# Low parts of output-product operands on POOL, and the scan's part added by accumulating transfers

## The chip, the cores and the metric

The kernel runs on one core of a Trainium2 chip. The metric is the device time of one execution in microseconds (us). The engines are TensorE (PE, with PEld for its weight loads), VectorE (DVE), ScalarE (ACT), GpSimd (POOL) and SyncE (SP). SP, ACT and POOL issue DMA transfers; each works through its own instructions in order, so an issue that waits holds up what stands behind it.

## The reference

One layer of a hybrid encoder for 512 tokens of width 2048, in float32: a bidirectional state-space scan and a multi-head latent attention run side by side from one input projection, and are merged:

```python
merged = jax.nn.sigmoid(g_ssm) * (y @ w_proj_ssm) + jax.nn.sigmoid(g_attn) * (o @ w_proj_attn)
return x + merged @ w_out
```

Here `y` is the scan's output and `o` that of attention, both 512x2048, and the two projections are 2048x2048. A final RMSNorm follows. The change concerns the two projections and the sum `merged`; everything ahead of them and behind them stays as it is.

## The kernel before, in words

**Precision.** Every float32 operand is held as two parts that TensorE multiplies at full rate: a high part (ACT's cast to the rounded type, L458) and a low part, the difference of the two (DVE's subtraction, L459). Where the negative is wanted (S2), L461 and L462 do the same with a scale of -1. One product of blocks is then three chains of matmuls: high by high (L604), high by the weights' low part (L605), low by high (L606). The function `split_into` makes both parts of 128x1024 elements. For weights the parts are called `wh` and `wl`, three buffers each; for operands they are kept whole (`S__13339` is S4 of the scan, `S__13418` is S3, `x__13505` is x22, `S__13044` S1 and `S__13049` S2; of attention's operands `x__13780` is x11, `x__13860` x12, `S__13948` S1, `S__14218` S4, `S__14317` S3 and `x__14398` x22).

**Strassen products.** Each projection is done by seven block products instead of eight, for each half of its columns. An operand is one of the blocks x11, x12, x22 or a sum S1 to S4 of blocks, which transfers have formed in DRAM before. A product runs over four chunks of weights: for each, the raw weights (or a column X or Y, or a sum of them) are split into `wh` and `wl`, and 12 matmuls follow, 48 in a product. The order in the scan's projection (`wps`) is P1 and P2 of both halves first, then, for each half, P5 (S1), P6 (S2), P3 (S4), P7 (S3), P4 (x22). Attention's projection (`wpa`) has P1, P5, P6, P2, P3, P7, P4 for each half. During P5, DVE also forms the column sums X+=Y (L721), and during P7 of the scan X is added up with raw weights loaded at that moment (L725, loads at L729).

**Operands while products run.** A table of hooks says after which product an operand is loaded (`L`, `LP`) and split (`C`, `CP`). The raw halves come through SP into a ring of three buffers, the same ring through which the raw weights come (`wraw`, with operands' halves named `xraw`). A buffer is free again when its low part has been made.

**What sets the order.** A scheduler orders the instructions of each engine by due times that the code sets by priorities; a step that is pinned (`keep_in_program_order`, in `CP` and `LP`) keeps its place in the order of the code among the other pinned ones. The splits of S4, S3 and x22 in the scan's projection, and of x22 in attention's, are not pinned before the change; the others in the table are.

**Gates and the merge.** When a block of the scan's projection is complete, DVE multiplies it by its gate (fetched by POOL a few products before) and POOL stores it to DRAM (`ms_d`). When a block of attention's is complete, DVE multiplies it by its gate (L1463), adds the scan's block (L1464), which POOL had fetched beside the gate into a buffer `ms` (L1456), and one product later TensorE transposes the result (`turn`, L1469) for the last projection.

Of the kernel before, what the change touches and what calls it, by code (L numbers as in the profile page):

```python
# [11 lines left out]
F32 = mybir.dt.float32  # L12
# [3 lines left out]
ALU = mybir.AluOpType  # L16
# [56 lines left out]
def build(tc, a):  # L73
    nc = tc.nc
    act, dve, pool, pe = nc.scalar, nc.vector, nc.gpsimd, nc.tensor
# [34 lines left out]
    def scratch(name, n=SEQ):  # L110
        return dr.tile([P, n], F32, name=name)
# [6 lines left out]
    zs_d, gs_d, ga_d, ms_d = ([[scratch(f"{n}{t}_{b}") for b in range(4)] for t in range(TT)]  # L118
                              for n in ("zs_d", "gs_d", "ga_d", "ms_d"))
# [167 lines left out]
    def put(dst, t):  # L287
        act.dma_start(dst, t)
# [116 lines left out]
    def st(name):  # L405
        return gp.tile([P, SEQ], F32, tag="st", bufs=3, name=name)
# [46 lines left out]

    def split_into(hi_, lo_, raw, sign=1):
        if sign == 1:
            i = act.copy(hi_, raw)  # L458
            dve.tensor_sub(lo_, raw, hi_.bitcast(F32))  # L459
        else:  # L460
            i = act.activation(hi_, raw, AF.Copy, scale=-1.0)  # L461
            dve.scalar_tensor_tensor(lo_, raw, -1.0, hi_.bitcast(F32), ALU.mult, ALU.subtract)  # L462
        return i

    def view4(t):
        return t.rearrange("p (k t) -> p k t", k=4)
# [8 lines left out]
    class Ops:  # L475
# [5 lines left out]
        def load(self, which, in_order=False):  # L481
            self.raws[which] = [raw_load(self.src[which], q, in_order) for q in range(2)]

        def split(self, which, op, in_order=False):
            for q, t in enumerate(self.raws.pop(which)):
                ks = slice(4 * q, 4 * q + 4)
                i = split_into(op[:, 0, ks], op[:, 1, ks], view4(t), -1 if which == "S2" else 1)
                if in_order:
                    tc.keep_in_program_order(i)
            self.view[which] = lambda s, j, i: op[:, s, j, i * P:(i + 1) * P]  # L490
# [42 lines left out]
    def w_split(raw):  # L533
        with tc.high_priority(offset=AHEAD):
            h = wp.tile([P, 1024], F32R, tag="wh", bufs=3, name="wh")
            l = wp.tile([P, 1024], F32R, tag="wl", bufs=3, name="wl")
            split_into(h, l, raw)
        return h, l
# [17 lines left out]
    def sum_tile(tag):  # L556

        if tag == "kk" or tag == "u" and kk:
            return kk.tile([P, SEQ], F32, tag="kk", bufs=2, name=tag)
        return part_.tile([P, SEQ], F32, tag=tag, bufs=2, name=tag)  # L560
# [11 lines left out]
    def after(n, f):  # L572
        later.append([n, f])
# [10 lines left out]
    def turn_bank(i):  # L584

        return SETS[used[1]][i]("turn")
# [24 lines left out]
    def product_rows(name, op, chunk, keep, each, pre):  # L611

        used.append((used[-1] + 1) % 4)
        bs = [b(name) for b in SETS[used[-1]]]
        for m in range(4):
            with tc.high_priority(offset=AHEAD):
                split_into(keep[0][:, m], keep[1][:, m], chunk(m))
        pre()
        for i in range(2):
            for j in range(8):  # L620
                xh, xl = op(0, j, i), op(1, j, i)
                wh, wl = (t[:, j // 2, j % 2 * 512:(j % 2 + 1) * 512] for t in keep)
                pe.matmul(bs[i], xh, wh, start=(j == 0), stop=False)
                pe.matmul(bs[i], xh, wl, start=False, stop=False)
                pe.matmul(bs[i], xl, wh, start=False, stop=(j == 7))
                yield 3
            each(i, bs[i])
# [791 lines left out]
    def place(shape, name, dt=F32R):  # L1419

        n = n_places[0] % 5
        n_places[0] += 1
        return xb.tile(shape, dt, tag="opb" if n else "opc", bufs=4 if n else 1, name=name)

    def slot(which):
        if which in ("x11", "x12"):
            return xa.tile([P, 2, 8, 256], F32R, tag="opa", bufs=2, name=f"{which}_")
        return place([P, 2, 8, 256], f"{which}_")

    y_ops, o_ops = Ops(yn_d), Ops(o_d)  # L1430

    def L(ops, w):
        return lambda: ops.load(w)

    def LP(ops, w):

        return lambda: ops.load(w, True)

    def C(ops, w):
        return lambda: ops.split(w, slot(w))  # L1440

    def CP(ops, w):

        return lambda: ops.split(w, slot(w), True)

    fetched = {}

# [4 lines left out]
    def fetch_pa(t, b):  # L1452
        fetched[t, b] = st("gate")
        pool.dma_start(fetched[t, b], ga_d[t][b])
        fetched["m", t, b] = sum_tile("ms")
        pool.dma_start(fetched["m", t, b], ms_d[t][b])  # L1456

    def done_ps(t, b, o):
        dve.tensor_mul(o, o, fetched.pop((t, b)))
# [1 line left out]

    def done_pa(t, b, o):
        dve.tensor_mul(o, o, fetched.pop((t, b)))  # L1463
        dve.tensor_add(o, o, fetched.pop(("m", t, b)))  # L1464

        def turn():
            tp = turn_bank(t % 2)
            for i in range(4):
                pe.transpose(tp[:, i * P:(i + 1) * P], o[:, i * P:(i + 1) * P], ident)  # L1469
            if b < 2:  # L1470
                o_ = st("turned")
                act.copy(o_, tp)
                d = m_d[f"x{t // 2 + 1}1"].rearrange("p (k t) -> p k t", k=8)
                put(d[:, 4 * b:4 * b + 4, t % 2 * P:(t % 2 + 1) * P], view4(o_))
            else:
                h, l = (m_op[f"x{t // 2 + 1}2"][:, s_, 4 * b - 8:4 * b - 4, t % 2 * P:(t % 2 + 1) * P] for s_ in range(2))
                act.copy(h, view4(tp))
                dve.tensor_sub(l, view4(tp), h.bitcast(F32))

        after(1, turn)  # L1480
# [3 lines left out]
    def m_place(*which):  # L1484
        def f():
            for w in which:
                op = m_op[w] = slot(w)
                m_ops.view[w] = lambda s, j, i, op=op: op[:, s, j, i * P:(i + 1) * P]
        return f
# [6 lines left out]
    def o_sums(n, i=1):  # L1496
        return lambda: [tc.keep_in_program_order(f()) for f in o_late[i][n]]

    wps = Strassen("wps", y_ops, -1, done_ps, fetch_ps, {
        (0, "P5"): [C(y_ops, "S4"), L(y_ops, "S3")],  # L1500
        (0, "P6"): [C(y_ops, "S3"), L(y_ops, "x22")], (0, "P3"): [C(y_ops, "x22")],
        (0, "P7"): [o_sums(2)], (0, "P4"): [LP(o_ops, "x11"), o_sums(3)],
        (1, "P5"): [CP(o_ops, "x11"), LP(o_ops, "x12"), o_sums(4)],
        (1, "P6"): [CP(o_ops, "x12"), LP(o_ops, "S1"), o_sums(5)],
        (1, "P3"): [CP(o_ops, "S1")], (1, "P7"): [LP(o_ops, "S2")], (1, "P4"): [CP(o_ops, "S2"), LP(o_ops, "S4")]})
    wpa = Strassen("wpa", o_ops, -1, done_pa, fetch_pa, {
        (0, "P1"): [CP(o_ops, "S4"), LP(o_ops, "S3")], (0, "P5"): [CP(o_ops, "S3"), LP(o_ops, "x22")],
        (0, "P6"): [C(o_ops, "x22")],
        (1, "P1"): [m_place("x11")], (1, "P5"): [m_place("x21")], (1, "P6"): [m_place("S1")],
        (1, "P2"): [m_place("x12"), L(m_ops, "x11")], (1, "P3"): [m_split("x11"), L(m_ops, "x21"), m_place("S2")],  # L1510
        (1, "P7"): [m_split("x21"), m_place("x22")], (1, "P4"): [m_place("S3")]})
# [7 lines left out]
    for hd in range(AH):  # L1519
# [24 lines left out]
        if hd == 12:  # L1544
            for w, tag in (("x11", "v_h"), ("x12", "v_l")):
                t = at.tile([P, TT, SEQ], F32R, tag=tag, bufs=2, name="yraw").bitcast(F32).rearrange("p a t -> p (a t)")
# [114 lines left out]
    for cg in range(2):  # L1661
        accs = [pa("f"), pa("f"), pb("f"), pb("f")] if cg == 1 else [mm("f"), mm("f"), mm("f"), pc("f")]
        for t in range(TT):
            o = res[t, cg] = sum_tile((("p1", "p5"), ("ms", "kk"))[cg][t // 2])
# [181 lines left out]
```

## Time and profile before

| | us |
|---|---|
| runs shown: median (lowest to highest) | 1981.22 (1973.48 to 1982.4) |
| profiled execution: time | 1973.34 |
| its span in the profile | 1971.6 |
| PE busy, idle in all | 1927.1, 44.5 |
| DVE busy | 1465.7 |
| ACT busy | 1028.9 |
| POOL busy | 249.3 |
| granted clock of TensorE | 0.998 |

Times in the profile count from the start of the span. The scan's projection runs from about 1470 us to 1635 us, attention's from there to about 1800 us. A row of a group gives the line, engine, operation, what is written and read, the shape and the count, then the busy time and the mean length of one in ns, and behind the last bar the engine's idle time just ahead of these instructions and what ended it. A row of the timeline begins with start and length in us.

### The profile page before, as it was taken

Reading aid. Unit: us, or ns where it says so; the run is one execution under the profiler, and the core shown is the slowest. Engines: PE = TensorE matmul, PEld = TensorE weight load, DVE = VectorE, ACT = ScalarE, POOL = GpSimd, SP = SyncE. Lnnn points to the kernel's source line nnn. Section 1 sums busy time; section 2 is a strip of 40 time slices with the busy share of each in tenths; the row PEclk is TensorE's granted clock in tenths of the full one; section 3 lists DMA queues with packets and bytes.
Section 4 is the critical chain, followed back from the end, with each engine's and each line's share of the span. In section 5 each row is a group of like instructions: output and inputs, shape, how many; then the busy total and the mean of one; then the engine's idle time right before and its main releaser. Section 6 shows DMA issues by size and latency. Waiting matters only on the chain.

```text
span 1971.6 us, 24488 instructions
## 1 busy us (share of the span) xinstructions
PE 1927.1 (98%) x8834; PEld 1590.0 (81%) x8834; DVE 1465.7 (74%) x2064; ACT 1028.9 (52%) x1527; POOL 249.3 (13%) x317
## 2 busy tenths in 40 slices
PE   7999999999999999999999999999999999999997
PEld 5888888888878888877788888888877787888886
DVE  7886676676759869788785557676776898879367
ACT  6444445444464856757747444444455455444353
POOL 0011001001112030030210211111021110100011
PEclk9999999999999999999999999999999999999999
DMA  6469669669654645665554867887388787847446
GB/s 216 167 203 255 165 167 245 155 179 246 144 175 146 202 125 162 205 206 189 158 159 139 243 176 201 210 222 201 105 217 309 235 280 276 281 157 242 168 85 161
DMA packets 170233, 383.27 MB, mean 194 GB/s; under 512 B 16704, under 2 KB 66944, under 8 KB 169920
## 3 DMA queue, kind: packets, MB, share of 16 engines
q1 hardware_dynamic: 103680, 234.02, 35.6%
q0 software_dynamic: 30912, 103.82, 23.5%
q10 hardware_dynamic: 35520, 43.87, 6.2%
q8 instruction: 69, 1.13, 0.2%
q14 instruction: 52, 0.43, 0.1%
HBM read 329.55 MB, written 98.17 MB: 217 GB/s over the span
## 4 chain that ended last, share of the span: by engine, by line
PE 78%; DVE 10%; DMA 6%; issue 3%; ACT 2%; POOL 0%; SPq 0%; ACTq 0%; DVEq 0%; POOLq 0%
PE P L605 11%; PE P L606 11%; PE P L604 11%; PE xbc L168 4%; PE xbc L169 4%; PE xbc L170 4%; PE za L170 2%; PE za L168 2%; PE za L169 2%; DVE sum L1135 2%; DVE wl L459 2%; PE qkv L168 1%; PE qkv L170 1%; PE qkv L169 1%; PE f L1613 1%
## 5 line engine op out<-in xcount | busy, mean ns | idle before, releaser
L458 ACT CAST wh<-X 128x1024 fp32r<-128x1024 f32 x164 | 172.4, 1054 | 197.6 <-PE P L606 149.6
L459 DVE TENSOR_TENSOR wl<-X,wh 128x1024 fp32r<-128x1024 f32 x164 | 199.7, 1222 | 85.7 <-ACT wh L458 85.2
L164 DVE TENSOR_TENSOR wl<-wraw,wh 128x1024 fp32r<-128x1024 f32 (+2 forms) x150 | 174.5, 1164 | 90.7 <-ACT wh L163 84.9
L163 ACT CAST wh<-wraw 128x1024 fp32r<-128x1024 f32 (+2 forms) x150 | 144.9, 967 | 121.6 <-PE xbc L169 34.4
L459 DVE TENSOR_TENSOR wl<-Y,wh 128x1024 fp32r<-128x1024 f32 x88 | 107.5, 1222 | 66.5 <-ACT wh L458 66.3
L458 ACT CAST wh<-Y 128x1024 fp32r<-128x1024 f32 x88 | 92.6, 1054 | 115.9 <-PE P L606 106.5
L168 PE MATMUL xbc<-h_h,wh 128*128 128x512 f32 x384 | 152.8, 398 | 0.0
L170 PE MATMUL xbc<-h_h,wl 128*128 128x512 f32 x384 | 149.8, 390 | 0.0
L169 PE MATMUL xbc<-h_l,wh 128*128 128x512 f32 x384 | 149.6, 390 | 0.0
L604 PE MATMUL P<-wh,h_h 128*128 128x512 f32 x384 | 149.4, 389 | 0.0
L605 PE MATMUL P<-wl,h_h 128*128 128x512 f32 x384 | 149.4, 389 | 0.0
L606 PE MATMUL P<-wh,h_l 128*128 128x512 f32 x384 | 149.4, 389 | 0.0
L458 ACT CAST wh<-wraw 128x1024 fp32r<-128x1024 f32 x68 | 71.7, 1055 | 110.6 <-PE P L606 60.1
L459 DVE TENSOR_TENSOR wl<-wraw,wh 128x1024 fp32r<-128x1024 f32 x68 | 83.0, 1221 | 59.7 <-ACT wh L458 59.7
L605 PE MATMUL P<-wl,S 128*128 128x512 f32 x288 | 112.1, 389 | 1.1 <-DVE wl L459 1.1
L604 PE MATMUL P<-wh,S 128*128 128x512 f32 x288 | 112.0, 389 | 0.0
L606 PE MATMUL P<-wh,S 128*128 128x512 f32 x288 | 112.0, 389 | 0.0
L170 PE MATMUL za<-h_h,wl 128*128 128x512 f32 x256 | 100.2, 391 | 2.5 <-DVE wl L164 2.5
L168 PE MATMUL za<-h_h,wh 128*128 128x512 f32 x256 | 101.5, 397 | 0.0
L169 PE MATMUL za<-h_l,wh 128*128 128x512 f32 x256 | 99.7, 389 | 0.0
L170 PEld LDWEIGHTS xbc<-h_h,wl 128*128 128x128 f32 x384 | 72.1, 188 | 15.6
L606 PEld LDWEIGHTS P<-wh,h_l 128*128 128x128 f32 x384 | 72.1, 188 | 15.0
(745 smaller groups left out, 5050.9 us busy)
## 6 DMA issues: line engine op xcount, KB each, us to landing
wraw<-wi SPq DMA_DIRECT2D x102, 512.0 KB, 3.7
T_wps<-wps POOLq DMA_DIRECT2D x32, 512.0 KB, 11.1
da<-da_d SPq DMA_DIRECT2D x64, 256.0 KB, 4.0
T_wpa<-wpa POOLq DMA_DIRECT2D x32, 512.0 KB, 9.3
wraw<-wps SPq DMA_DIRECT2D x24, 512.0 KB, 6.2
wraw<-wo SPq DMA_DIRECT2D x20, 512.0 KB, 3.6
xbc_d<-xbc ACTq DMA_DIRECT2D x24, 256.0 KB, 2.8
wraw<-wun SPq DMA_DIRECT2D x16, 384.0 KB, 5.2
```

What stands on the lines that cost most here:

```text
L163: act.copy(h, raw)
L164: dve.tensor_sub(l, raw, h.bitcast(F32))
L168: pe.matmul(out, wh, xh, start=start, stop=False)
L169: pe.matmul(out, wh, xl, start=False, stop=False)
L170: pe.matmul(out, wl, xh, start=False, stop=stop)
L458: i = act.copy(hi_, raw)
L459: dve.tensor_sub(lo_, raw, hi_.bitcast(F32))
L604: pe.matmul(bs[i], xh, wh, start=(j == 0), stop=False)
L605: pe.matmul(bs[i], xh, wl, start=False, stop=False)
L606: pe.matmul(bs[i], xl, wh, start=False, stop=(j == 7))
L1135: dve.tensor_tensor_scan(sums[-1], flat(da), mask, 0.0, ALU.add, ALU.mult)
L1613: pe.matmul(acc, mh, wh, start=(start and k == 0), stop=False)
```

## The change

`split_into` and `split` get an argument for the engine of the subtraction. A new hook `CQ` splits with the low part on POOL and the cast pinned. It takes the place of `C` and `CP` for S4, S3 and x22 of both projections and for x11, x12 and S1 of attention: nine operands of two halves, 18 subtractions of 128x1024. The loads of S3 in the scan's projection become pinned. S2 (with the scale of -1) stays on DVE. The scan's block is no longer fetched and added by DVE; an accumulating POOL transfer adds it from DRAM onto the finished block, after the gate's multiplication and ahead of the turn.

```diff
-    def split_into(hi_, lo_, raw, sign=1):
+    def split_into(hi_, lo_, raw, sign=1, by=dve):
         if sign == 1:
             i = act.copy(hi_, raw)
-            dve.tensor_sub(lo_, raw, hi_.bitcast(F32))
+            by.tensor_sub(lo_, raw, hi_.bitcast(F32))
...
-    def CP(ops, w):
-
-        return lambda: ops.split(w, slot(w), True)
+    def CP(ops, w, by=dve):
+
+        return lambda: ops.split(w, slot(w), True, by)
+
+    def CQ(ops, w):
+        return CP(ops, w, pool)
...
-        fetched["m", t, b] = sum_tile("ms")
-        pool.dma_start(fetched["m", t, b], ms_d[t][b])
...
-        dve.tensor_add(o, o, fetched.pop(("m", t, b)))
+        pool.dma_start(o, ms_d[t][b], accum_op=ALU.add)
...
     wps = Strassen("wps", y_ops, -1, done_ps, fetch_ps, {
-        (0, "P5"): [C(y_ops, "S4"), L(y_ops, "S3")],
-        (0, "P6"): [C(y_ops, "S3"), L(y_ops, "x22")], (0, "P3"): [C(y_ops, "x22")],
+        (0, "P5"): [CQ(y_ops, "S4"), LP(y_ops, "S3")],
+        (0, "P6"): [CQ(y_ops, "S3"), LP(y_ops, "x22")], (0, "P3"): [CQ(y_ops, "x22")],
...
-        (1, "P5"): [CP(o_ops, "x11"), LP(o_ops, "x12"), o_sums(4)],
-        (1, "P6"): [CP(o_ops, "x12"), LP(o_ops, "S1"), o_sums(5)],
-        (1, "P3"): [CP(o_ops, "S1")], (1, "P7"): [LP(o_ops, "S2")], (1, "P4"): [CP(o_ops, "S2"), LP(o_ops, "S4")]})
+        (1, "P5"): [CQ(o_ops, "x11"), LP(o_ops, "x12"), o_sums(4)],
+        (1, "P6"): [CQ(o_ops, "x12"), LP(o_ops, "S1"), o_sums(5)],
+        (1, "P3"): [CQ(o_ops, "S1")], (1, "P7"): [LP(o_ops, "S2")], (1, "P4"): [CP(o_ops, "S2"), LP(o_ops, "S4")]})
     wpa = Strassen("wpa", o_ops, -1, done_pa, fetch_pa, {
-        (0, "P1"): [CP(o_ops, "S4"), LP(o_ops, "S3")], (0, "P5"): [CP(o_ops, "S3"), LP(o_ops, "x22")],
-        (0, "P6"): [C(o_ops, "x22")],
+        (0, "P1"): [CQ(o_ops, "S4"), LP(o_ops, "S3")], (0, "P5"): [CQ(o_ops, "S3"), LP(o_ops, "x22")],
+        (0, "P6"): [CQ(o_ops, "x22")],
```

Three places show how the order moves. On DVE at the start of P5 in the scan's first half, before:

```order
L462 SCALAR_TENSOR_TENSOR S__13049<-xraw,S__13049 128x1024
L459 TENSOR_TENSOR S__13339<-xraw,S__13339 128x1024
L462 SCALAR_TENSOR_TENSOR S__13049<-xraw,S__13049 128x1024
L459 TENSOR_TENSOR wl<-X,wh 128x1024
L459 TENSOR_TENSOR S__13339<-xraw,S__13339 128x1024
L721 TENSOR_TENSOR X<-X,Y 128x1024
L459 TENSOR_TENSOR wl<-X,wh 128x1024 x2
```

And now:

```order
L462 SCALAR_TENSOR_TENSOR S__13049<-xraw,S__13049 128x1024 x2
L459 TENSOR_TENSOR wl<-X,wh 128x1024
L721 TENSOR_TENSOR X<-X,Y 128x1024
L459 TENSOR_TENSOR wl<-X,wh 128x1024
L679 TENSOR_TENSOR p_13243<-kk,P2b 128x512
```

The two halves of S4 no longer stand among P5's first weights. On ACT, from S2's casts to those of x22, before:

```order
L461 ACTIVATE S__13049<-xraw 128x1024
L458 CAST S__13339<-xraw 128x1024
L461 ACTIVATE S__13049<-xraw 128x1024
L458 CAST wh<-X 128x1024
L458 CAST S__13339<-xraw 128x1024
L458 CAST wh<-X 128x1024
L458 CAST S__13418<-xraw 128x1024
L458 CAST wh<-X 128x1024 x2
L458 CAST S__13418<-xraw 128x1024
L458 CAST x__13505<-xraw 128x1024
```

And now, where L567 is the eviction of P5's result:

```order
L461 ACTIVATE S__13049<-xraw 128x1024 x2
L458 CAST wh<-X 128x1024 x6
L567 COPY p_13335<-P_13257 128x512
L567 COPY p_13337<-P_13258 128x512
L458 CAST wh<-X 128x1024
L458 CAST S__13339<-xraw 128x1024 x2
L458 CAST wh<-X 128x1024
L458 CAST S__13418<-xraw 128x1024
L458 CAST wh<-Y 128x1024
L458 CAST S__13418<-xraw 128x1024
L458 CAST wh<-Y 128x1024 x3
L458 CAST x__13505<-xraw 128x1024 x2
```

S4's casts now follow P5's eviction, and S3's and x22's stand between the Y columns, which are P3's weights. On POOL, among the transfers for the sums of attention's operands, the gates and the stores of finished blocks, before:

```order
L1406 DMA o_S_221<-o_x_220 128x512
L1450 DMA gate<-gs_d_1_154 128x512
L1460 DMA ms_d_1_178<-ms 128x512
L1450 DMA gate<-gs_d_1_158 128x512
L1460 DMA ms_d_1_182<-ms 128x512
```

And now:

```order
L1406 DMA o_S_221<-o_x_220 128x512
L1453 DMA gate<-gs_d_1_154 128x512
L459 TENSOR_TENSOR S__13339<-xraw,S__13339 128x1024 x2
L459 TENSOR_TENSOR S__13418<-xraw,S__13418 128x1024 x2
L459 TENSOR_TENSOR x__13505<-xraw,x__13505 128x1024 x2
L1461 DMA ms_d_1_178<-ms 128x512
L1453 DMA gate<-gs_d_1_158 128x512
```

Six subtractions stand in a row ahead of the next store and the next gate's fetch. Those of x11, x12 and S1 stand in the same way in the second half, and those of attention's S4, S3 and x22 in a row ahead of the first accumulating transfer.

More of the change, by code (lines that the diff above doesn't have):

```diff
@@ L482, in load, with split @@
             self.raws[which] = [raw_load(self.src[which], q, in_order) for q in range(2)]
-        def split(self, which, op, in_order=False):
+        def split(self, which, op, in_order=False, by=dve):
             for q, t in enumerate(self.raws.pop(which)):
                 ks = slice(4 * q, 4 * q + 4)
-                i = split_into(op[:, 0, ks], op[:, 1, ks], view4(t), -1 if which == "S2" else 1)
+                i = split_into(op[:, 0, ks], op[:, 1, ks], view4(t), -1 if which == "S2" else 1, by)
                 if in_order:
```

## The prediction

> **What bounds the kernel now.** I read the page's busy times first, then the busy time of each engine in the stretch between the starts of the products that the change touches, then what TensorE waited for there, then the single rows in which POOL and DVE meet.
>
> ```profile
> span 1971.6 us, 24488 instructions
> PE 1927.1 (98%) x8834; PEld 1590.0 (81%) x8834; DVE 1465.7 (74%) x2064; ACT 1028.9 (52%) x1527; POOL 249.3 (13%) x317
> ```
>
> PE is busy for 98% of the span, so little is left to win: 44.5 us of idle time in all. The next view cuts the scan's and attention's output products at their starts: the columns are from and to, length, then busy time and count of PE, PEld, DVE, ACT and POOL, then clock, DMA share and GB/s. The rows are P5, P6, P3 and P7 of the scan's first half; P6, P3 and P7 of its second half; and P5, P6 and P2 of attention's first half.
>
> ```profile
> core 0: us, PE busy (x) PEld busy (x) DVE busy (x) ACT busy (x) POOL busy (x), PEclk, DMA share, GB/s
> 1518.68:1531.79 13.11, 11.59 (x50) 9.04 (x49) 13.11 (x14) 8.81 (x9) 0.95 (x2) 1.00 0.48 168
> 1531.79:1543.14 11.35, 11.19 (x50) 8.93 (x48) 9.11 (x9) 4.23 (x5) 3.05 (x5) 1.00 0.84 199
> 1543.14:1555.86 12.72, 11.45 (x50) 8.93 (x48) 9.39 (x10) 6.00 (x6) 0.00 (x0) 1.00 0.49 142
> 1555.86:1567.78 11.92, 11.35 (x50) 8.85 (x48) 8.53 (x10) 4.21 (x4) 1.18 (x3) 1.00 0.93 347
> 1590.27:1601.14 10.87, 10.87 (x49) 9.01 (x48) 9.53 (x9) 8.39 (x9) 2.42 (x4) 1.00 0.82 229
> 1601.14:1612.03 10.89, 10.89 (x50) 9.01 (x49) 9.99 (x11) 6.01 (x6) 0.00 (x0) 1.00 0.94 298
> 1612.03:1623.35 11.32, 11.32 (x50) 8.86 (x48) 9.65 (x11) 4.21 (x4) 1.13 (x2) 1.00 0.94 327
> 1646.42:1657.31 10.89, 10.89 (x50) 9.01 (x49) 10.31 (x10) 7.25 (x9) 0.00 (x0) 1.00 0.56 211
> 1657.31:1668.23 10.92, 10.92 (x49) 8.82 (x48) 8.96 (x8) 7.45 (x8) 0.00 (x0) 1.00 0.41 128
> 1668.23:1680.50 12.27, 11.48 (x50) 9.07 (x50) 12.27 (x14) 5.27 (x5) 0.00 (x0) 1.00 0.74 236
> ```
>
> An undisturbed product takes 10.88 us (48 matmuls; 10.87 to 10.89 in three rows), so a chunk of 12 matmuls, which needs one new `wl`, lasts 2.72 us. Over 10.88 stand P5 by 2.2 us, P3 by 1.8, P7 by 1.0 and P2 by 1.4; the ten rows lose 7.5 us together. That is the ceiling of any gain here, 0.4% of the span. DVE is busy for all of P5 and P2 and for 8.5 to 10.3 us elsewhere.
>
> ```profile
> L605 PE MATMUL P<-wl,S__13044 128*128 128x512 f32 x32 | 12.7, 396 | 1.5 <-DVE wl L459 1.5
> L605 PE MATMUL P<-wl,S__13339 128*128 128x512 f32 x32 | 12.6, 393 | 0.9 <-DVE wl L459 0.9
> L605 PE MATMUL P<-wl,S__13418 128*128 128x512 f32 x32 | 12.9, 404 | 0.6 <-DVE wl L459 0.6
> L605 PE MATMUL P<-wl,x__13505 128*128 128x512 f32 x32 | 12.7, 396 | 0.9 <-DVE wl L459 0.9
> ```
>
> Whenever PE stops here, a `wl`, the low part of the weights made by DVE, is what ended the wait (S__13044 is S1 of P5). DVE's order is therefore what bounds the stretch, and the change works on the right engine.
>
> **What a POOL low part costs.** No 128x1024 subtraction on POOL is in the trace. The nearest rows, of a start, a length and an instruction, except the last, which is a group:
>
> ```profile
> 573.51 1.26 POOL L1023 TENSOR_TENSOR c_l<-CT,c_h 128x512 fp32r<-128x512 f32 x1 [36.44 <-DMA xs<-xbc_d]
> 689.26 1.81 POOL L1023 TENSOR_TENSOR c_l<-CT,c_h 128x512 fp32r<-128x512 f32 x1 [68.91 <-ACT c_h L1022]
> 733.80 2.98 POOL L1088 TENSOR_TENSOR yo<-yo,tmp 128x512 f32<-128x512 f32 x2 [5.02 <-DVE tmp L1087]
> 735.56 2.31 DVE L164 TENSOR_TENSOR wl<-wraw,wh 128x1024 fp32r<-128x1024 f32 x1
> 871.37 2.56 POOL L1088 TENSOR_TENSOR yo<-yo,tmp 128x512 f32<-128x512 f32 x2
> 872.72 2.30 DVE L164 TENSOR_TENSOR wl<-wraw,wh 128x1024 fp32r<-128x1024 f32 x1 [2.19 <-ACT wh L163]
> L1370 POOL TENSOR_TENSOR small<-sm__9863 x1: 189/189/189, 1178.2 to 1178.2; 128x1 f32<-128x1 f32 x1
> ```
>
> c_l is the same operation at half the width, 1.26 us in the one that took least. A one-column instruction takes 0.19, so a doubled width is 0.19 + 2 x (1.26 - 0.19) = 2.33 us, which I take. The lowest it could be is 1.26 (if width cost nothing), the highest twice the 1.81 of the other c_l quoted, 3.6 (it has a wait in it). [...]
>
> The same rows show the second cost. In the pair at 733.80 POOL ends at 736.78 and the DVE split ends at 737.87, 1.09 us later; in the pair at 871.37 POOL ends at 873.93 and the split at 875.02, again 1.09 later. A split takes about 1.1 to 1.22 us, so both splits did nothing until POOL had finished: DVE and POOL take turns for whole instructions. [...] Moving a split to POOL therefore doesn't take it off DVE's time. It replaces a turn of 1.22 by one of 2.33.
>
> **The change, part by part.** Eighteen low parts leave DVE (9 operands of two halves) and become POOL instructions. Their times now:
>
> ```profile
> L459 DVE TENSOR_TENSOR S__13339<-xraw,S__13339 x2: 1217/1222/1226, 1516.8 to 1520.2; 128x1024 fp32r<-128x1024 f32 x2
> L459 DVE TENSOR_TENSOR S__13418<-xraw,S__13418 x2: 1212/1215/1218, 1535.1 to 1537.4; 128x1024 fp32r<-128x1024 f32 x2
> L459 DVE TENSOR_TENSOR x__13505<-xraw,x__13505 x2: 1220/1223/1226, 1538.5 to 1545.4; 128x1024 fp32r<-128x1024 f32 x2
> L459 DVE TENSOR_TENSOR x__13780<-xraw,x__13780 x2: 1217/1218/1219, 1593.2 to 1594.3; 128x1024 fp32r<-128x1024 f32 x2
> L459 DVE TENSOR_TENSOR x__13860<-xraw,x__13860 x2: 1217/1222/1226, 1596.6 to 1599.5; 128x1024 fp32r<-128x1024 f32 x2
> L459 DVE TENSOR_TENSOR S__13948<-xraw,S__13948 x2: 1215/1216/1216, 1606.4 to 1607.6; 128x1024 fp32r<-128x1024 f32 x2
> L459 DVE TENSOR_TENSOR S__14218<-xraw,S__14218 x2: 1217/1219/1221, 1649.6 to 1653.6; 128x1024 fp32r<-128x1024 f32 x2
> L459 DVE TENSOR_TENSOR x__14398<-xraw,x__14398 x2: 1218/1222/1226, 1660.0 to 1666.0; 128x1024 fp32r<-128x1024 f32 x2
> ```
>
> *P5, gain.* S4's two halves (1516.8 and 1520.2) stand today ahead of P5's first `wl` and of its first column sum. Pinned later, they leave that place: two turns of 1.22 less in a row full of DVE work. PE waited 1.5 us there for `wl`; I take a gain of 1.7 (bounds 1.5 and 2.2).
>
> *P6 and P3 of the first half.* ACT's order puts the casts of S4 behind P5's evictions, so S4, S3 and x22 all fall in these two products, six POOL turns of 2.33 = 14.0 us. DVE is busy for 9.11 + 9.39 = 18.5 us there, of which four splits (S3, x22) leave, 4.9. The turns add up to 27.6 us, against 24.1 us that the two products take today: +3.5. That is a floor, since turns alternate: a `wl` that is wanted every 2.72 us stands behind a turn of 2.33, and with the split itself (1.1) that is 3.4. Four POOL turns (S3, x22) stand in P3 alone, and each makes its chunk late by up to 0.7; two such are counted, 1.5. Together +5.
>
> *P6 and P3 of the second half.* x11, x12 and S1 stand here already, so six splits (7.3 us) leave and 14.0 come: 9.53 + 9.99 - 7.3 + 14.0 = 26.2 against 21.8, +4.4; with the same 1.5 for order, +6.
>
> *P7 of both halves.* The raw halves of operands share a ring of three buffers with the raw weights that P7 adds into X (L725), and a buffer is now given back by POOL.
>
> ```profile
> 1552.81 6.42 DMA wraw<-wps
> 1559.25 1.22 DVE L725 TENSOR_TENSOR X<-X,wraw 128x1024 f32<-128x1024 f32 x1 [3.60 <-DMA wraw<-wps]
> ```
>
> The first of these loads is issued at 1552.81 and lands at 1559.2, and DVE waits 3.6 us for it, with P7's third `wl` queued behind it. x22's last half is done at 1546.6 today; by six turns in a row it is done near the end of P3, up to 10 us later, and the second and third weight loads with it. I take +3 per P7 (bounds 0, if the queue's own earlier loads still set the time, and 6.4, a whole load): +6.
>
> *Attention's P5, P6 and P2.* S4, S3 and x22: 10.31 + 8.96 - 7.3 + 14.0 = 26.0 against 21.8 for P5 and P6: +4.2, say +4; P2 itself is full of DVE work and neither gains nor loses by it.
>
> *Accumulating transfers.* Sixteen loads of `ms` and sixteen DVE additions go, and sixteen accumulating POOL transfers come.
>
> ```profile
> L1464 DVE TENSOR_TENSOR p<-p,ms 128x512 f32<-128x512 f32 x12 | 8.2, 684 | 0.0
> ms<-ms_d POOLq DMA_DIRECT2D x16, 256.0 KB, 5.4
> big<-x POOLq DMA_DIRECT2D x8, 256.0 KB, 5.9
> L1688 POOL DMA_DIRECT2D big<-x x8 | 7.0, 1170 | 34.1 <-DVE big L737 27.2 <-DVE big L656 5.5 <-DVE big L651 1.5
> ```
>
> The additions are 16 x 0.68 = 11 us of DVE, after 1668 and with nothing waiting for them (0.0 idle behind), so I count no gain; the bound is P2's 1.4. The nearest accumulating transfer (`big<-x`) lands 5.9 us after its issue, and its issue takes 1.17: 7.1 us from the gate multiplication to the data. The turn comes one product later, 10.88 us: covered by 3.8. Where the second of a pair waits for a DVE turn that cover shrinks, and if it were gone the transfer would cost up to 7 us. I take +1 for the last of them.
>
> *Sum:* -1.7 + 5 + 6 + 6 + 4 + 1 = +20.3 us. The profiled execution took 1973.34 us (1971.6 of span and 1.7 around it), so 1993.6; I say 1993. The three runs shown go from 1973.48 to 1982.4 with a median of 1981.22: the profiled one is at their fast end, and a median may stand up to 8 us above my frame.
>
> **The rivals.** *Hidden.* A chunk has 2.72 - 1.22 = 1.5 us of slack. If a POOL turn took less than that, each would fit between two `wl`. The row at 573.51 is 1.26, so this holds if width costs little; one column at 0.19 speaks against it. Then the gain of P5 and the 1 of the transfers are left, with perhaps half of one P7: 1972 to 1979. Chance 0.18.
>
> *No turns, a gain.* If the subtraction of POOL ran beside DVE's, 18 splits and 16 additions would leave DVE for nothing, 33 us, and PE would win what it loses to `wl`: at most 7.5, 1966. The two meetings quoted speak against it. Chance 0.08.
>
> *Later still.* If the accumulating transfers land after the turn is due, in POOL's queue behind subtractions or slower than `big<-x`, each of eight pairs costs 2 or 3 us more: 1993 + 20 = 2013. It decides from a landing time of 10.9 us. Only attention's first pairs stand near POOL work, which speaks against it. Chance 0.1.
>
> **How the numbers follow.** The forecast itself (turns are exclusive, sum +10 to +30) has 0.64. Its own range is 1983 to 2005. The range takes in the upper end of "hidden" and most of "later still": 1975 to 2011. What a measurement of this kernel can tell from no change is about 0.5%, 9.9 us. Slower by more: 0.64 + 0.1, less a small part of the forecast that falls short, 0.73. Within: 0.19. Faster: 0.08.
>
> **What would show it.** A POOL L459 row near 2.3 us alone and near 3.4 behind a DVE split; DVE splits of 2 to 3.5 us in 1531 to 1690; PE idle before L605 in P3 and P7 of several us, where it is 0.6 to 0.9 now; P5's 13.1 us near 11.3. Wrong would be: POOL rows under 1.5 us; DVE splits staying at 1.22 beside POOL; P3 under 13 us in both halves. For the transfers: a `p<-ms_d` issue landing within 7 us, and PE not waiting at the turn's transposes.

## The result, and the profile after

The changed kernel takes 2006.87 us in the median of its runs, the kernel before 1978.27 in as many. The ratio is 1.0146, with a 95% interval of 1.013 to 1.0163: it is slower by 28.9 us. One of its five runs took 3975.4 us, and one run of an experiment below 5036.37 us; executions as far off as these are left out of the ratios. The forecast was 1993 with a range of 1975 to 2011 and slower as the likeliest side. The time is in the range, but the loss is about 1.4 times the sum of 20.3 us, and it is made up otherwise.

First the same rows as before, of the changed kernel: the head of its page with the span and the busy time of each engine, and then its stretches between the starts of products, in the prediction's order (P5, P6, P3, P7; P6, P3, P7; P5, P6, P2).

```profile
span 2005.4 us, 24491 instructions
PE 1940.6 (97%) x8834; PEld 1599.7 (80%) x8834; DVE 1460.2 (73%) x2030; ACT 1029.0 (51%) x1527; POOL 308.9 (15%) x335
```

```profile
core 0: us, PE busy (x) PEld busy (x) DVE busy (x) ACT busy (x) POOL busy (x), PEclk, DMA share, GB/s
1520.06:1530.94 10.88, 10.88 (x49) 8.89 (x48) 10.85 (x13) 4.81 (x5) 1.14 (x3) 1.00 0.47 164
1530.94:1542.58 11.64, 11.19 (x49) 8.93 (x48) 7.92 (x5) 6.38 (x8) 9.63 (x7) 1.00 0.65 135
1542.58:1559.16 16.58, 13.15 (x49) 9.90 (x48) 14.10 (x10) 7.98 (x8) 11.83 (x4) 0.90 0.62 190
1559.16:1570.04 10.88, 10.88 (x49) 9.01 (x48) 8.86 (x10) 4.22 (x4) 1.54 (x3) 1.00 1.00 379
1592.20:1603.20 11.00, 11.00 (x50) 8.93 (x48) 7.21 (x6) 8.38 (x9) 9.56 (x6) 1.00 0.57 151
1603.20:1620.20 17.00, 13.70 (x49) 10.52 (x48) 14.36 (x9) 6.21 (x6) 11.01 (x5) 0.82 0.75 234
1620.20:1631.54 11.34, 11.34 (x50) 9.31 (x48) 10.44 (x11) 3.90 (x4) 2.25 (x4) 0.96 0.99 368
1654.76:1667.13 12.37, 11.18 (x49) 8.94 (x48) 11.58 (x7) 7.07 (x8) 5.83 (x2) 1.00 0.56 207
1667.13:1680.11 12.98, 11.04 (x49) 8.82 (x47) 4.97 (x4) 7.43 (x8) 10.22 (x4) 1.00 0.32 103
1680.11:1694.95 14.84, 12.79 (x48) 10.24 (x49) 14.28 (x15) 5.26 (x5) 0.28 (x1) 0.89 0.66 208
```

Against the rows of before, P5 is 2.2 us shorter (10.88 instead of 13.11: it loses nothing any more) and P7 of the first half 1.0 shorter. P3 is 3.9 us longer in the first half (16.58 instead of 12.72) and 6.1 in the second (17.00 instead of 10.89). Attention's P5, P6 and P2 are 1.5, 2.1 and 2.6 longer. The 2.1 of P6 are in the main one stop at its very end, from 1678.17 to 1680.11, in which PE already waits for the first `wh` of P2. Note the clock: in P3 of the second half PE is busy for 13.70 us with work that takes 10.88 elsewhere, and the granted clock is 0.82. Of the 6.1 us lost there, 3.3 are idle and 2.8 are slow matmuls. The same slow stretch reaches into the P7 behind it (0.96).

How the turns of POOL and DVE look in P3 of the first half, in the changed kernel's timeline (start, length, instruction; first POOL, then DVE):

```profile
1535.81 5.83 POOL L459 TENSOR_TENSOR S__13339<-xraw,S__13339 128x1024 fp32r<-128x1024 f32 x2 [2.01 <-ACT S__13339 L458]
1541.61 6.72 POOL L459 TENSOR_TENSOR S__13418<-xraw,S__13418 128x1024 fp32r<-128x1024 f32 x2
1548.30 6.11 POOL L459 TENSOR_TENSOR x__13505<-xraw,x__13505 128x1024 fp32r<-128x1024 f32 x2
```

```profile
1546.00 1.27 DVE L737 TENSOR_TENSOR p<-p,P 128x512 f32<-128x512 f32 x2
1547.19 1.69 DVE L651 TENSOR_TENSOR p<-p,p 128x512 f32<-128x512 f32 x1
1548.81 3.37 DVE L459 TENSOR_TENSOR wl<-Y,wh 128x1024 fp32r<-128x1024 f32 x1
1552.11 2.85 DVE L651 TENSOR_TENSOR p<-p,p 128x512 f32<-128x512 f32 x1
```

POOL works without a gap from 1535.81 to 1554.41. A `wl` beside it takes 3.37 us instead of 1.22, and the small sum L651 takes 1.69 and 2.85 instead of 0.68. The two L737 ahead of them, which read one operand from PSUM (P), have POOL's subtraction of S3 beside them all the time and take 1.27 us together, no longer than without POOL (0.68 each in the mean before the change).

The two POOL low parts that DVE did not hold up are the last of attention's (x22, in a stretch in which DVE waited for a transfer). Their row among the changed kernel's POOL groups gives 2.37 us each, where the estimate was 2.33.

```profile
L459 POOL TENSOR_TENSOR x__14398<-xraw,x__14398 128x1024 fp32r<-128x1024 f32 x2 | 4.7, 2375 | 0.0
```

The other part of the loss is at the turns. Before the change PE never waited there; now it waits 12.9 us for the accumulating transfers, in four stops. These are the group rows of the kernel before and of the changed one, then the changed kernel's stretches of two of these turns (8 transposes) and of the products behind them:

```profile
L1469 PE MATMUL turn<-cst,p 128*128 128x128 f32 x48 | 6.2, 272 | 0.0
```

```profile
L1470 PE MATMUL turn<-cst,p 128*128 128x128 f32 x48 | 7.6, 290 | 12.9 <-DMA p<-ms_d 12.9
```

```profile
1705.83:1708.93 3.10, 1.01 (x9) 0.77 (x8) 2.46 (x3) 1.53 (x2) 0.00 (x0) 1.00 1.05 372
1708.93:1721.55 12.62, 12.62 (x51) 10.20 (x50) 5.27 (x7) 3.75 (x4) 2.91 (x4) 0.86 0.92 267
...
1733.34:1740.35 7.01, 1.36 (x9) 1.12 (x8) 3.00 (x5) 1.53 (x2) 1.73 (x3) 0.77 0.94 248
1740.35:1753.04 12.69, 12.69 (x50) 10.25 (x49) 5.58 (x6) 4.34 (x5) 1.44 (x2) 0.86 0.57 160
```

These two stops are paid twice: the product behind takes 12.6 to 12.7 us, all of it busy, at a granted clock of 0.86, where the same products take about 11.0 elsewhere. A third pair, from 1797.57, reads 4.20 and 12.59 us; behind the fourth stop, of 2.02 us, the product takes its usual 11.0. With three slow products, 12.9 + 3 x 1.6 = 17.7 us. The sum of what the rows lost in the products above is -2.2 + 0.3 + 3.9 - 1.0 + 0.1 + 6.1 + 1.5 + 2.1 + 2.6 = 13.4. Together that is 31, against 33.8 between the two profiled executions (2007.17 and 1973.34).

The four stops do not have one cause. Each ended when the second transfer of its pair landed. For that transfer, the table has the time from the end of the product that completed the block to the end of DVE's multiplication and to the issue on POOL, and then how long the landing took (us, from the changed kernel's timelines and its chain of waits):

| stop of PE, and its end | product's end | to multiplied | to issue | landing |
|---|---|---|---|---|
| 2.09, 1708.52 | 1694.95 | 4.4 | 4.7 | 8.8 |
| 5.65, 1739.59 | 1721.55 | 4.5 | 11.3 | 6.7 |
| 3.13, 1801.35 | 1786.58 | 3.3 | 4.5 | 10.3 |
| 2.02, 1816.98 | 1797.57 | 11.7 | 12.3 | 7.1 |

In the first and the third the landing is long. In the fourth the multiplication itself comes late. In the second, the longest, both are ordinary, but the issue stands 6.7 us behind the multiplication: on POOL a gate's fetch is ahead of it, and does not go before 1731.42.

```profile
1731.42 0.57 POOL L1457 DMA_DIRECT2D gate<-ga_d  x1 [7.14 <-issue]
1732.80 0.85 POOL L1465 DMA_DIRECT2D p<-ms_d  x1 [0.80 <-issue]
```

Gates and the turned blocks share one ring of three buffers in the program (`st`), and by the trace the store of a turned block landed at 1730.89, just before the fetch. Issued right behind its multiplication (1726.1), with the same 6.7 us, the transfer would by estimate have landed at 1732.8, ahead of the turn at 1733.34. No run takes this ring away, so this part is read from traces alone.

### The profile page after: what moved, and what is told of

It is laid out like the page before. It is cut to its first block, busy times and chain, and to the rows that moved or that the text cites. A ratio compares the mean times of both kernels' runs of the same rounds, so it can differ in the third digit from the quotient of the medians.

```text
span 2005.4 us, 24491 instructions
## 1 busy us (share of the span) xinstructions
PE 1940.6 (97%) x8834; PEld 1599.7 (80%) x8834; DVE 1460.2 (73%) x2030; ACT 1029.0 (51%) x1527; POOL 308.9 (15%) x335
## 4 chain that ended last, share of the span: by engine, by line
PE 78%; DVE 9%; DMA 5%; issue 5%; ACT 2%; POOL 1%; SPq 0%; ACTq 0%; POOLq 0%; DVEq 0%
PE P L605 10%; PE P L606 10%; PE P L604 10%; PE xbc L168 4%; PE xbc L169 3%; PE xbc L170 3%; PE za L170 2%; PE za L168 2%; PE za L169 2%; DMA p<-ms_d 2%; DVE sum L1135 2%; PE qkv L168 1%; PE qkv L170 1%; PE qkv L169 1%; PE f L1615 1%
## 5 line engine op out<-in xcount | busy, mean ns | idle before, releaser
L459 DVE TENSOR_TENSOR wl<-Y,wh 128x1024 fp32r<-128x1024 f32 x88 | 116.5, 1327 | 73.7 <-ACT wh L458 73.7
L605 PEld LDWEIGHTS P<-wl,h_h 128*128 128x128 f32 x384 | 72.1, 188 | 15.1
```

The costliest lines, as they stand in the source:

```text
L459: by.tensor_sub(lo_, raw, hi_.bitcast(F32))
```

## The experiments

Each ratio is against the kernel before, timed on the same chip, with its 95% interval; us are the ratio times 1975.5, about the median of the kernel before in these runs. The theory after the result had two independent parts, the turns of POOL on DVE's time and the landing of the accumulating transfers; the rivals were the sum on record, and the pinned order as the cause.

### The transfers alone

```diff
-        fetched["m", t, b] = sum_tile("ms")
-        pool.dma_start(fetched["m", t, b], ms_d[t][b])
...
-        dve.tensor_add(o, o, fetched.pop(("m", t, b)))
+        pool.dma_start(o, ms_d[t][b], accum_op=ALU.add)
```

> The kernel before, with the accumulating transfers alone: no load of ms, no DVE addition, sixteen accumulating POOL transfers; all low parts on DVE in the old order. Prediction's theory: +1 us, PE does not wait at the turn. Theory from the changed kernel's trace: PE waits at four or five of the eight turns for 2 to 6 us each and runs the next matmuls at half rate after each wait, together +12 to +18 us (ratio 1.006 to 1.009). Rival: the waits of the changed kernel came only because low parts on POOL made attention's first half late, then here +0 to +3 us.

Measured: ratio 1.0082 (1.0063 to 1.0101), +16 us. The transfers alone cost more than half of the whole loss, with no low part on POOL. PE waits 7.4 us at the turns by the row of its groups, and one product behind them again takes 12.6 us. These make 9.0 us in this one execution. It is 16.1 us longer than the profiled one of the kernel before, but 4.0 of these lie ahead of 1501 us, where nothing was changed.

```profile
L1467 PE MATMUL turn<-cst,p 128*128 128x128 f32 x48 | 7.3, 279 | 7.4 <-DMA p<-ms_d 7.4
```

The chain of waits of this run shows the worst place (start, length, what ran):

```profile
1769.96 0.61 DVE p L1461
1770.62 1.72 issue
1772.36 0.49 POOL p L1462
1772.91 0.41 POOL gate L1454
1773.45 10.29 DMA p<-ms_d
1783.79 0.72 PE turn L1467 x4
```

The product ended at 1768.95, so the turn was due at about 1779.9. The gate's multiplication comes 1 us after that end, the issue 3.4 to 4.5 us after it, and the landing takes 10.3 us.

### The low parts on POOL alone

The change with the two hunks above taken back.

> The change without the accumulating transfers: 18 low parts on POOL, the scan's part fetched and added by DVE as before. Prediction's theory: +19 us (ratio 1.0097), with 3 us each in P7 of both halves. Theory from the changed kernel's trace: +12 to +16 us, of which P3 of the two halves has 4 and 6 and attention's P5, P6 and P2 some 6, P5 of the scan gains 2, and P7 loses nothing. If the transfers were the whole cost: +0.

Measured: 1.0066 (1.0048 to 1.0084), +13 us, inside what the trace of the changed kernel gave and below the sum on record. P3 takes 16.20 and 17.13 us in this run, as in the changed kernel. With the run before it, 13 + 16 = 29 us, the whole loss: within the intervals, some 4 us for each, the two parts add up.

### The order without POOL

```diff
     def CQ(ops, w):
-        return CP(ops, w, pool)
+        return CP(ops, w, dve)
```

with DVE's additions put back.

> The same pinned order as the changed kernel, but every low part on DVE and the scan's part added by DVE. If POOL's turns are the cost of P3: -2 to +2 us, with P3 of both halves under 13 us. If the pinned order itself (S3 and x22 falling into P3) is the cost: +8 to +12 us, P3 near 16 us as in the changed kernel.

Measured: 0.9996 (0.9984 to 1.0009). The pinned order is not the cause. The rows of its stretches are P3 and P7 of the first half and P3 of the second:

```profile
1546.57:1557.61 11.04, 11.04 (x50) 8.93 (x48) 10.49 (x12) 7.41 (x8) 0.00 (x0) 1.00 0.72 223
1557.61:1572.23 14.62, 12.81 (x49) 10.07 (x48) 12.18 (x13) 4.20 (x4) 2.17 (x4) 0.88 0.88 315
1604.87:1615.75 10.88, 10.88 (x49) 9.01 (x48) 10.23 (x11) 6.02 (x6) 0.00 (x0) 1.00 0.90 303
```

P3 takes 11.04 and 10.88, as long as an undisturbed product. Most of what P5 and P3 of the first half gain, P7 gives back (14.62, before 11.92).

### Half as long turns

```diff
-            by.tensor_sub(lo_, raw, hi_.bitcast(F32))
+            if by is dve:
+                by.tensor_sub(lo_, raw, hi_.bitcast(F32))
+            else:
+                for k in range(2):
+                    by.tensor_sub(lo_[:, 2 * k:2 * k + 2], raw[:, 2 * k:2 * k + 2], hi_[:, 2 * k:2 * k + 2].bitcast(F32))
```

> As the kernel with low parts on POOL and DVE's additions, but each POOL low part is made by two instructions of half the width (about 1.2 to 1.3 us each instead of 2.35). If the length of one turn against a chunk's slack of 1.5 us is what makes weights late: most of the loss in P3 goes, +3 to +7 us over the kernel before instead of +12 to +16. If the summed time of the turns is what counts: no better than with whole instructions, +12 to +17.

Measured: 1.0056 (1.0039 to 1.0074), +11 us, not to be told from the +13 of whole instructions. In P3 of the first half the stop of 3.1 us is gone, two of 0.9 stand there instead, and P3 takes 13.37 us instead of 16.20. But P3 of the second half keeps a stop of 2.6 us (16.29), and while attention's P5 is 1.5 us shorter than with whole instructions, both P7 and attention's P6 and P2 are 0.4 to 1.0 longer. So shorter turns help in places but did not bring the total down to the +3 to +7 that the first of the two expectations gave. That the summed time of the turns is what counts would fit; why the time comes back elsewhere is not shown. In this run POOL's half instructions took 1.3 to 2.1 us in the mean of a group, where the shortest c_l of this width took 1.26 before; that they wait for DVE would fit (rows of its groups from 1500 to 1720):

```profile
L463 POOL TENSOR_TENSOR x__13509<-xraw,x__13509 128x512 fp32r<-128x512 f32 x4 | 8.4, 2139 | 0.0
L463 POOL TENSOR_TENSOR x__13868<-xraw,x__13868 128x512 fp32r<-128x512 f32 x4 | 5.0, 1300 | 0.0
```

### A transfer that nobody waits for

```diff
-        dve.tensor_mul(o, o, fetched.pop((t, b)))
-        pool.dma_start(o, ms_d[t][b], accum_op=ALU.add)
+        g = fetched.pop((t, b))
+        dve.tensor_mul(o, o, g)
+        pool.dma_start(g, ms_d[t][b], accum_op=ALU.add)
```

> As the kernel with accumulating transfers alone, but each transfer adds the scan's block onto the gate's buffer, which nobody reads any more, instead of onto the finished block; the scan's part is thereby left out of the sum. Same transfers, same DVE work, but the turn waits for the gate's multiplication only. If it is the wait for the landing that costs (and the slow matmuls behind each stop): the cost of 16 us goes, -2 to +3 us against the kernel before. If the transfers themselves disturb (POOL's queue, the gate buffers, DMA load): it stays at +10 to +16 us.

This kernel leaves the scan's part out of the sum. Measured: 1.0023 (1.0006 to 1.0039), +4.5 us instead of +16. The same transfers, issued at the same places, with the turn no longer waiting for them, as the group row of this run shows:

```profile
L1468 PE MATMUL turn<-cst,p 128*128 128x128 f32 x48 | 6.2, 272 | 0.0
```

So about 12 of the 16 us (16.2 - 4.5, each good to some 3.5) are the wait for the transfers and the slow matmuls behind it. The last 4.5 (1 to 8 by the interval) are above the expected -2 to +3 and stay unexplained. In the profiled execution 2.0 us stand in one product (12.98 from 1775.81, before 10.98): ACT waited 5.41 us there for a load (`xraw<-m_x`), and the next `wl` was late behind it. Whether the transfers held up this load is not shown.

### The three groups of low parts, one at a time

Each is the kernel before with one group by `CQ` and the other groups as they were.

The second group, x11, x12 and S1 of attention, was pinned already, so only the engine changes:

```diff
-        (1, "P5"): [CP(o_ops, "x11"), LP(o_ops, "x12"), o_sums(4)],
-        (1, "P6"): [CP(o_ops, "x12"), LP(o_ops, "S1"), o_sums(5)],
-        (1, "P3"): [CP(o_ops, "S1")], (1, "P7"): [LP(o_ops, "S2")], (1, "P4"): [CP(o_ops, "S2"), LP(o_ops, "S4")]})
+        (1, "P5"): [CQ(o_ops, "x11"), LP(o_ops, "x12"), o_sums(4)],
+        (1, "P6"): [CQ(o_ops, "x12"), LP(o_ops, "S1"), o_sums(5)],
+        (1, "P3"): [CQ(o_ops, "S1")], (1, "P7"): [LP(o_ops, "S2")], (1, "P4"): [CP(o_ops, "S2"), LP(o_ops, "S4")]})
```

> The kernel before with six low parts on POOL alone: x11, x12 and S1 of attention, which were pinned already and whose place in the order does not change. So only the engine differs. Theory of turns, by the trace of the changed kernel: P3 of the scan's second half loses 6 us, +5 to +8 us in all. By the sum on record, +6 in P6 and P3 and +3 in P7: +9. If the engine alone were harmless and the order were the cause: 0 to +2.

Measured: 1.0015 (1.0004 to 1.0027), +3 us: less than both theories gave. Its P3 and P7 in the second half:

```profile
1605.50:1622.00 16.50, 13.11 (x50) 10.00 (x49) 14.16 (x9) 6.40 (x7) 11.14 (x5) 0.90 0.76 232
1622.00:1632.88 10.88, 10.88 (x50) 9.01 (x48) 9.84 (x11) 4.22 (x4) 1.17 (x2) 1.00 0.98 374
```

P3 does lose 5.6 us, as in the changed kernel. Against that, what comes behind it is shorter: P7 takes 10.88 instead of 11.32, and P4 and attention's P1 and P2 gain 0.2 to 0.5 each, 1.5 in all. The 4 us that are left lie inside the interval (0.8 to 5.3). That a stop of PE gives the transfers in flight more time to land would explain the gain; no run shows it by itself.

The first group, S4, S3 and x22 of the scan:

> The kernel before with the first group of six low parts alone on POOL and pinned: S4, S3 and x22 of the scan. By the sum on record: -1.7 + 5 + 3 (P7) = +6.3 us. By the changed kernel's trace: P3 loses 4 us more than before, P5 gains 2, P7 gains up to 1: +1 to +3. If the three groups share the 13 us that all eighteen cost, with 3 for the second group: +4 to +5.

Measured: 1.0007 (0.9998 to 1.0016), +1.4 us, by the trace's estimate and not by the sum on record. In its trace P5 gains 1.4, P3 loses 3.9 and P7 gains 1.0.

The third group, S4, S3 and x22 of attention:

> The kernel before with the third group alone on POOL: S4, S3 and x22 of attention. By the sum on record: +4 us. By the changed kernel's trace, in which P5, P6 and P2 lose 1.5, 2.1 and 4.0 us against 0, 0 and 1.4 before: +6. If these waits came only because the groups ahead had made DVE late: +0 to +2.

Measured: 1.0039 (1.0025 to 1.0054), +7.7 us, the largest of the three; the groups ahead were not needed for it. The three groups give 1.4 + 3.0 + 7.7 = 12.1 us, the eighteen together 13. Why this one is worst is told by what SP's queue waited for in this run from 1640 to 1685 (in us, times, longest), and by DVE's timeline:

```profile
SPq L470 <- POOL S__14218 L459: 12.1, 2, 9.2
SPq L470 <- POOL S__14317 L459: 8.6, 1, 8.6
```

```profile
1650.27 3.31 DVE L721 TENSOR_TENSOR X<-X,Y 128x1024 f32<-128x1024 f32 x1
1653.51 3.40 DVE L459 TENSOR_TENSOR wl<-X,wh 128x1024 fp32r<-128x1024 f32 x1
...
1671.40 2.51 DVE L725 TENSOR_TENSOR X<-X,wraw 128x1024 f32<-128x1024 f32 x1 [5.47 <-DMA wraw<-wpa]
```

Two things happen. POOL's turns lengthen the column sum and a `wl` in P5 to 3.3 and 3.4 us. And SP waits 20.7 us with its next raw loads until POOL has given back a buffer of the ring; P2's first raw weights therefore land so late that DVE sits idle for 5.5 us. The trace tells them apart by place: P5 is 1.9 us longer than before, and PE stands still for 1.95 us at the end of P6, for P2's first `wh`, and for 2.02 in P2, for its `wl`. With the slow matmuls behind these stops (0.43 us each instead of 0.23, and a granted clock of 0.78 in P2), P6 and P2 are 5.5 us longer together. A larger ring, which would test this, was not tried.

### S4 alone, on either engine

```diff
-        (0, "P5"): [C(y_ops, "S4"), L(y_ops, "S3")],
+        (0, "P5"): [CQ(y_ops, "S4"), L(y_ops, "S3")],
```

> The kernel before with the two halves of the scan's S4 alone on POOL, pinned as in the change. P5 gains 2 us as in the changed kernel; P6, in which the two turns fall, has 9.1 us of DVE work in 11.35, less than S3's and x22's splits that stand there, so that two turns of 2.35 fill it: theory of turns -1 to +4 us. If turns on POOL cost nothing where only two fall into a product: -2.

Measured: 0.9999 (0.9986 to 1.0012). The same with `CP` in place of `CQ`, so on DVE:

> The kernel before with the scan's S4 pinned and split by DVE, nothing on POOL: the one part of the change that takes work out of P5's start. P5 gains 1.5 to 2 us. If that gain stays, -2 us; if P7 gives it back, as in the run with every pin and no POOL (P7 lost 3.75 us there, 1.0 before), -1 to +1.

Measured: 0.9993 (0.998 to 1.0006). Both do what the change wanted in P5 (PE's wait for `wl` in S1's products falls from 1.5 to 0.4 us with the pin), and neither moves the time beyond its interval. The gain is given back, but not in P7, as was expected (11.09 and 11.06 us, before 11.92): in both traces it is P4 of the first half that grows, from 11.61 to 16.39 and 14.03 us. The trace with POOL is that of the slowest of its twelve runs (1984.35, median 1976.5). Neither can be called faster than the kernel before; no version here beats it.

### The gate's multiplication first

```diff
-        dve.tensor_mul(o, o, fetched.pop((t, b)))
-        pool.dma_start(o, ms_d[t][b], accum_op=ALU.add)
+        with tc.high_priority(offset=AHEAD):
+            dve.tensor_mul(o, o, fetched.pop((t, b)))
+            pool.dma_start(o, ms_d[t][b], accum_op=ALU.add)
```

> As the kernel with accumulating transfers alone, but the gate's multiplication and the transfer are given the priority that weight splits have, so that DVE comes to them up to one or two instructions earlier. If the landing, 13 us and more after the product's end against 10.9, is late by the whole chain: the 16 us shrink by 1 to 4 us, and the turn still waits. If DVE's place for the multiplication is the whole cause: +3 us or less against the kernel before.

Measured: 1.0079 (1.0062 to 1.0096), +15.6 us: no change from +16. So a higher priority for the multiplication saves nothing. The test is a weak one: against the run with the transfers alone, the second multiplication of a pair comes 1 to 2 us earlier behind its product in five pairs and no earlier in the other three. The chain of this run's longest stop (3.31 us) has the wait of the gate's fetch for a buffer:

```profile
1696.32 5.53 DMA m_x<-turned
1702.42 0.09 POOL gate L1454
1702.97 6.88 DMA p<-ms_d
```

The multiplication was done at 1699.0, the transfer behind the gate's fetch was issued 4 us later, and it landed at 1709.86 for a turn that began at 1705.99.

## Why the prediction was right, and where its steps were wrong

**The direction and its reason.** The sum said slower, since a POOL low part is a turn of 2.33 us in place of one of 1.22. That held: 2.37 us where POOL was alone, 3.37 for a DVE split behind it, P3 of 16.6 and 17.0 us, and no loss in P3 when the same order runs without POOL. Not every DVE instruction beside POOL took longer: two L737, which have a PSUM operand, took 1.27 us together, as without POOL (0.68 each), and two L651 with both operands in SBUF took 1.69 and 2.85 instead of 0.68. In the prediction's reading of PE's waits, "whenever" was a little too much: 0.3 us ahead of the first half's P3 were ended by a `wh`.

**P5, -1.7.** Right: 13.11 to 10.88, -2.2.

**P6 and P3, +5 and +6.** About right as to place: +4.2 in the first half and +6.2 in the second, by the rows of the changed kernel. But a count of turns was only part of the reason: 3.4 and 3.3 us of the two P3 are idle time, and of what PE's work took beyond 10.88 (2.3 and 2.8 us) the larger part is due to the reduced clock behind the stop (0.90 and 0.82 over the two P3), which the prediction did not have.

**P7, +3 twice.** Wrong. The step failed where it made the second and third weight loads late "with" x22's last half: P7 lost nothing (10.88) or as much as before (11.34 against 11.32), because P3 itself had become longer and the loads landed within that time. In the first half DVE's wait for the first of them is 2.22 us instead of 3.60, and it lands 2.0 us after the start of P7 instead of 3.4. The ring of three buffers did cost time, in attention's P2, where the prediction counted nothing.

**Attention's P5, P6 and P2, +4.** Too small: 1.5, 2.1 and 2.6 in the changed kernel, 7.7 us for this group alone. The turns cost less than the +4 (P5's 1.5; P6's 2.1 are already the wait for P2's weights). The step "P2 itself neither gains nor loses" is the one that failed; its raw weights came late through the ring.

**Low parts in all.** The prediction's terms give -1.7 + 5 + 6 + 6 + 4 = 19.3; measured, 13.

**The accumulating transfers, +1.** The mis-sized term: 16 us. Its step of "7.1 us from the gate multiplication to the data", covered by 3.8, failed. (The 5.9 us in it run from the start of the issue, so that the 1.17 of the issue were counted twice; that error is on the safe side.) Four things were missing. First, the 10.88 us start at the product's end, not at the multiplication; in the changed kernel the pair's issues stand 3.4 and 4.7 us behind that end (1694.95), by its timeline of POOL:

```profile
1698.37 0.90 POOL L1465 DMA_DIRECT2D p<-ms_d  x1 [17.98 <-DVE p L1464]
1698.96 0.88 POOL L1457 DMA_DIRECT2D gate<-ga_d  x1
1699.69 1.05 POOL L1465 DMA_DIRECT2D p<-ms_d  x1
```

and the chain of waits has the landing of the second:

```profile
1699.69 8.79 DMA p<-ms_d
```

Second, this landing took 8.8 us where 5.9 was taken from `big<-x`, the median of eight landings from 4.3 to 8.2 us at another time of the kernel (the median of the new transfers onto `p` is 6.8). 4.7 + 8.8 = 13.5 us, against the 10.9 at which the turn is due. Third, POOL's order: a gate's fetch that waits for a buffer holds up the transfer behind it, as in the stop of 5.65 us. Fourth, behind three of the four stops the next matmuls were slow (a granted clock of 0.86 over the product). The rival "later still" had the mechanism (a landing past 10.9 us, through POOL's queue or a slower transfer), but got a chance of 0.1, on the argument that only the first pairs stand near POOL's subtractions: the run with the transfers alone shows that no subtraction is needed.

**The total.** +20.3 came near to the measured +28.9 by luck: two errors of opposite sign, 6 us too much for the low parts and 15 too little for the transfers. The side was right for a reason that held, the turns; the size was not.

## What to carry to other kernels

Moving work between two engines that take turns, as POOL and DVE did here with these splits, does not add an engine: count the new turn against the old one (2.37 us against 1.22), and remember that the engine you relieve still pays for it (3.37 us for a `wl` that took 1.22). Replacing an early load and a cheap addition by an accumulating transfer moves the transfer from before the data are ready to after it, onto the path (4.7 us to the issue and 8.8 to the landing at the first stop here, with the turn due after 10.9): measure the cover from the moment the data come into being, with the landing time of that place and with what stands ahead of it in the issuing engine's order. And a short stop of TensorE can cost more than its length, where the clock falls behind it: the product behind the stop of 2.09 us took 12.62 us, at a granted clock of 0.86, instead of about 11.0.

## What the runs showed of the hardware that was not expected

After the stop of 2.09 us TensorE ran at half its rate for 3.41 us (0.43 us a matmul instead of 0.23). In the clock records of the changed kernel, which begin at 27 us, the granted clock is either 1.00 or 0.50, and all its half-rate stretches lie on one raster: they start at 1037.35, 1552.76, 1614.20, 1682.47, 1709.78, 1737.08, 1801.94 and 1996.50 us, whole multiples of 3.413 us apart. The last one runs past the end of the span; each of the others lasts 3.41 or 6.83 us. So two stops of about the same length had different prices. The rows are two intervals of that raster around the stop of 2.09 us (turn at 1705.83) and two around the stop of 2.02 us, which began at 1814.96 and has a part in the interval ahead of the ones shown; the number ahead of the DMA share is the granted clock:

```profile
1706.37:1709.78 3.41, 1.32 (x9) 1.14 (x9) 3.03 (x4) 1.76 (x3) 0.33 (x1) 1.00 1.03 384
1709.78:1713.19 3.41, 3.41 (x10) 2.64 (x9) 0.82 (x2) 0.02 (x1) 0.91 (x2) 0.50 1.06 320
...
1815.59:1819.01 3.42, 2.03 (x11) 1.77 (x12) 2.81 (x5) 1.09 (x3) 1.43 (x2) 1.00 1.04 346
1819.01:1822.42 3.41, 3.41 (x17) 2.81 (x16) 2.06 (x3) 1.05 (x1) 0.00 (x0) 1.00 1.01 335
```

The first stop lies in one interval, in which PE is busy for 1.32 us, and the next interval runs at half clock. The second is split between two, PE is busy for 2.03 us in the fuller one, and the clock stays.

It is the same in the two traces of the kernel before and the changed one, cut into such intervals from the start of their clock records on (25 and 27 us). After an interval at full clock in which PE was busy for less than 1.5 us (0.00 to 1.47; seven in the changed kernel, one in the kernel before) the next one was always at half clock; after 2.02 us or more it never was. Between these lie three intervals of the changed kernel, behind short stops near 573, 1037 and 1130 us, with 1.83, 1.74 and 1.65 us busy: only the second was followed by half clock. In the run with the low parts alone PE has 4.34 us of idle time in P3 of the first half (11.86 busy of 16.20) and no slow matmuls there, at a granted clock of 1.00; that its stops are split between intervals would fit. Where the raster lies differs between the two executions: the one half-rate stretch in the trace of the kernel before starts at 1964.08 us, half an interval off the raster of the changed kernel. So the time of stages that were not changed can differ too: the stretch at 1037.35 has no counterpart in the kernel before, and costs some 1.7 us by estimate (half of 3.41); the first P5 starts at 1520.06 us in the changed kernel and at 1518.68 in the kernel before.
